# Hybrid attention encoder layer: the output projection turned round, and the second chunk's matmuls ordered by token block

## The chip, the cores and the metric

The kernel runs on one core of a Trainium2 chip. The metric is the device time of one execution in microseconds (us).

## The reference, cut to what matters

One encoder layer is applied to a prompt of 1024 tokens and to a sample of 256 tokens, each with 16 meta tokens ahead; the model width is 2048.

```python
def encoder_layer(h, norm_w, w_in, ..., w_out, rope_tabs):
    u = rms_norm(h, norm_w) @ w_in
    qa, ka, va, za, qb, kb, vb, zb = jnp.split(u, split_points(), axis=-1)
    ...
    ya = global_gqa(qa, ka, va) * jax.nn.silu(za)              # heads 0 to 7
    yb = neighbourhood_attention(qb, kb, vb, rpb) * jax.nn.silu(zb)   # heads 8 to 15
    y = jnp.concatenate([ya, yb], axis=-1) @ w_out             # 2048 x 2048
    return h + y
```

The meta tokens' rows are dropped from the output, so the output projection covers 1280 tokens.

## The kernel before

**Precision.** TensorE works on float32 numbers split in two parts, high and low (`split`, L56: ScalarE copies the high part, L58; VectorE subtracts it, L59). A product is three matmuls: high by high, high by low, low by high (L206 to L208 and L945 to L947).

**First chunk** (`chunk1`): 512 tokens, namely the sample, 240 prompt tokens and the meta tokens. For each strip of 128 columns of w_in, `strips` (L173) accumulates 16 tiles of 128 features, w as weights, tokens moving in one block of 496 or 512. Attention of the sample runs between strips. Beside it, `w_sums` (L536) computes four matrices of differences of w_out's quarters and leaves them in DRAM (`td`).

**Second chunk** (`chunk2`): the other 784 tokens in two blocks of 512 and 272. `strips` goes through four groups of four feature tiles; inside a group it takes tile by tile, inside a tile each job (strip), and inside a job both token blocks: three matmuls of 512, then three of 272. Between strips run attention blocks: global heads (`attend`, L317) and, for the local heads, four strips of 256 queries each (`attend_strip`, L412). The last strip projected is v of the last local head. Each block's result goes to DRAM by `put_y` (L300, store L315) in tensors `yd`, one a head, 128 features by 1280 tokens.

**Output projection** (`outproj`, L990). It follows Strassen's scheme in Winograd's form: seven products of half-size matrices in the order 1, 2, 5, 6, 7, 3, 4. The halves of y are the global heads and the local heads by two halves of 640 tokens; those of w_out are 1024 by 1024. Product 1 takes the global heads of the first half, product 2 the local heads of the first half. A product has eight steps, one for each 128 output features: 8 heads x 2 token blocks x 3 matmuls, 48 matmuls with w as weights and 320 tokens moving (`products`, L936). `y_load` and `y_operand` (L871, L885) bring one head's 640 tokens and split them; eight such tiles serve a product, 16 buffers (`ym`) hold two products. `w_load` and `w_operand` (L901, L912) bring and split the weights of a step two or three steps ahead. `out_sums` (L950) adds the product into the running sums U and V (`us`, `vs`) or into an output tile `o` that already holds the residual x (`x_load`, L921); `store` writes it.

**What sets the order.** All DMAs are issued by SyncE's queue (SP), in order; every engine executes its queue in order. The order of the queues is chosen ahead of the run by a list scheduler with the program order as priority. From the start of product 2 on, `in_order` (L860) pins each engine to the program's order. The last local head's four strips are emitted after steps 0 to 3 of product 1. The pools of the output projection (`us`, `raw3`, `ym`) take the memory on the right side that x of the second chunk (16 tiles of 6.25 KB a partition) and the scales beside it (6.1 KB) leave; a buffer waits for the tiles that lay there. The pools `yr`, `ysp`, `w2`, `raw2`, `vs`, `ob` take the place of the attention's pools once its last strip is done.

Of the kernel before, what the change touches and what calls it, by code (L numbers as in the profile page):

```python
# [20 lines left out]
P = 128  # L21
DM = 2048
# [24 lines left out]
TH = (NP + NS) // 2  # L47
QA, KA, VA, ZA, QB_, KB, VB, ZB = 0, 8, 10, 12, 20, 28, 36, 44
# [3 lines left out]
class Kern:  # L52
# [120 lines left out]
    def strips(self, jobs, getx):  # L173
# [4 lines left out]
        for c in range(KT // WCH):  # L178
# [21 lines left out]
            for k in range(WCH):  # L200
                kt = c * WCH + k
                x = getx(kt)
                for (wh, wl), ps, (_, blocks, _) in zip(ws, out, jobs):
                    for p, (_, n), (xh, xl) in zip(ps, blocks, x):
                        first, last = kt == 0, kt == KT - 1
                        nc.tensor.matmul(p[:, :n], wh[:, k, :], xh[:, :n], start=first, stop=False)  # L206
                        nc.tensor.matmul(p[:, :n], wh[:, k, :], xl[:, :n], start=False, stop=False)  # L207
                        nc.tensor.matmul(p[:, :n], wl[:, k, :], xh[:, :n], start=False, stop=last)  # L208
# [91 lines left out]
    def put_y(self, po, tot, zs, ydst):  # L300
# [14 lines left out]
        nc.sync.dma_start(ydst, y[:].rearrange("p (g r) -> p g r", g=4) if len(ydst.shape) == 3 else y[:])  # L315
# [220 lines left out]
    def w_sums(self):  # L536
# [6 lines left out]
        for s in range(8):  # L543
            for i in range(0, 8, WCH):
                q = {}
                for n, c, j in (("12", 8 + s, i), ("11", s, i), ("22", 8 + s, 8 + i), ("21", s, 8 + i)):
                    r = self.xr.tile([P, WCH, P], F32, tag="xr", name="wq")
                    nc.sync.dma_start(r[:], w[c][:, j:j + WCH, :])
                    q[n] = r[:]
# [7 lines left out]
                for n, p in (("11", 5), ("12", 7), ("22", 6), ("21", 4)):  # L557
                    nc.sync.dma_start(self.td[s][p][:, i:i + WCH, :], q[n])
                yield

    def chunk1(self):
# [86 lines left out]
        def run(h, q, z, k, v, vm, tab):  # L648
            k, km = k
            ydst = self.yd[h][:, NP:]  # L650
# [33 lines left out]
    def chunk2(self):  # L684
# [115 lines left out]
        def run_block(h, b, q, z, k, v, tab):  # L800
            k, km = k
            v, vm = v
            if tab is not None:
                c = slice(64 * b, 64 * b + 64)
                q, qf = q
                self.attend_strip(q, qf, strips_of(z[:])[:, :, c], k, km, v[b], vm[:], tab, b,
                                  strips_of(self.yd[h][:, :NP])[:, :, c])
# [63 lines left out]
    def y_load(self, p, k):  # L871

        def half(h, t):
            r = self.yr.tile([P, TH], F32, tag="xr", name="yr")
            self.nc.sync.dma_start(r[:], self.yd[h][:, TH * t:TH * t + TH])
            return r[:]

        if p in (1, 2, 4):
            t = self.ym.tile([P, 2, TH], F32R, tag="ym", name="ym", align_bytes=ALIGN)
            self.nc.sync.dma_start(t[:, 1, :].bitcast(F32), self.yd[k if p == 1 else 8 + k][:, TH * (p == 4):][:, :TH])  # L880
            return t
        return [half(*x) for x in {7: [(k, 0), (k, 1)],
                                   5: [(k, 1), (8 + k, 1)], 6: [(k, 0)], 3: [(8 + k, 0)]}[p]]

    def y_operand(self, p, k, r):  # L885
        nc = self.nc
        if p in (1, 2, 4):
            self.split(r[:, 0, :], r[:, 1, :], r[:, 1, :].bitcast(F32))
# [4 lines left out]
        else:  # L893
            v = self.ysum[k][:]
            a, b, op = {5: (r[0], r[-1], ALU.add), 6: (v, r[0], ALU.subtract), 3: (r[0], v, ALU.subtract)}[p]
            nc.vector.tensor_tensor(out=v, in0=a, in1=b, op=op)
        t = self.ym.tile([P, 2, TH], F32R, tag="ym", name="ym", align_bytes=ALIGN)
        self.split(t[:, 0, :], t[:, 1, :], v)
        return t

    def w_load(self, p, s):  # L901
        src = {1: lambda: self.io["w_out"][s][:, :8, :], 2: lambda: self.io["w_out"][s][:, 8:, :],
               3: lambda: self.io["w_out"][8 + s][:, 8:, :]}.get(p, lambda: self.td[s][p][:])()
        out = []
        self.nwl += 1
        for i, pool in enumerate((self.raw, (self.raw2, self.raw3)[self.nwl % 2])):
            r = pool.tile([P, WCH, P], F32, tag="raw", name="wr")
            self.nc.sync.dma_start(r[:], src[:, WCH * i:WCH * i + WCH, :])
            out.append(r)
        return out  # L910

    def w_operand(self, raws):  # L912
        ws = []
        for i, r in enumerate(raws):
            wh = self.ws[i].tile([P, WCH, P], F32R, tag="wh", name="wh")
            wl = self.ws[i].tile([P, WCH, P], F32R, tag="wl", name="wl")
            self.split(wh[:], wl[:], r[:])
            ws += [(wh[:, k, :], wl[:, k, :]) for k in range(WCH)]
        return ws

    def x_load(self, p, s):  # L921

        nc, io = self.nc, self.io
        if p not in (2, 7, 3, 4):
            return None
        o = self.ob.tile([P, TH], F32, tag="o", name="o")
        c, half = {2: (s, 0), 7: (8 + s, 1), 3: (8 + s, 0), 4: (s, 1)}[p]
        if half == 0:
            nc.sync.dma_start(o[:, :C1P], io["x1"][:, c, NS:NS + C1P])
            nc.sync.dma_start(o[:, C1P:], io["x2"][:, c, :TH - C1P])  # L930
        else:
            nc.sync.dma_start(o[:, :NP - TH], io["x2"][:, c, TH - C1P:])
            nc.sync.dma_start(o[:, NP - TH:], io["x1"][:, c, :NS])
        return o

    def products(self, ws, ys):  # L936
        nc = self.nc
        B = TH // 2
        ps = self.pq.tile([P, 2, 512], F32, tag="pq", name="pq")
        for k in range(8):  # L940
            wh, wl = ws[k]
            yh, yl = ys[k][:, 0, :], ys[k][:, 1, :]
            for b in range(2):
                o = slice(B * b, B * b + B)
                nc.tensor.matmul(ps[:, b, :B], wh, yh[:, o], start=k == 0, stop=False)  # L945
                nc.tensor.matmul(ps[:, b, :B], wh, yl[:, o], start=False, stop=False)  # L946
                nc.tensor.matmul(ps[:, b, :B], wl, yh[:, o], start=False, stop=k == 7)  # L947
        return ps[:, :, :B]

    def out_sums(self, p, s, ps, o):  # L950

        nc = self.nc

        def two(t):
            return t[:].rearrange("p (b n) -> p b n", b=2)
# [4 lines left out]
        if p == 1:  # L960
            self.U[s] = self.us.tile([P, TH], F32, tag="u", name="u")
            nc.scalar.copy(two(self.U[s]), ps)
            return None
        if p == 5:
            self.V[s] = self.vs.tile([P, TH], F32, tag="v", name="v")
            nc.scalar.copy(two(self.V[s]), ps)
            return None
        if p == 6:
            add(two(self.U[s]), ps, two(self.U[s]))
            add(self.V[s][:], self.V[s][:], self.U[s][:])  # L970
            return None
        if p in (2, 4):
            add(o[:], o[:], self.U[s][:])
            add(two(o), two(o), ps, ALU.add if p == 2 else ALU.subtract)
            return o, s, int(p == 4)
        add(o[:], o[:], self.V[s][:])
        add(two(o), ps, two(o))
        if p == 7:
            add(two(self.U[s]), ps, two(self.U[s]))
        return o, 8 + s, int(p == 7)  # L980

    def store(self, o, c, half):
        nc, io = self.nc, self.io
        if half == 0:
            nc.sync.dma_start(io["yp"][:, c, :TH], o[:])
        else:
            nc.sync.dma_start(io["yp"][:, c, TH:], o[:, :NP - TH])
            nc.sync.dma_start(io["ys"][:, c, :], o[:, NP - TH:])

    def outproj(self, end_attention):  # L990
        self.U, self.V = {}, {}
        order = (1, 2, 5, 6, 7, 3, 4)
        N = 8 * len(order)

        def step(n):
            return order[n // 8], n % 8

        yr, ys, wr, ws, x, out = {}, {}, {}, {}, {}, {}

        def get(d, n, f, *a):  # L1000
            if n not in d and n < N:
                d[n] = f(*step(n), *a)


        for n in range(8):
            yr[n] = self.y_load(*step(n))
            ys[n] = self.y_operand(*step(n), yr.pop(n))
            if n == 0:
                for i in range(2):
                    get(wr, i, self.w_load)  # L1010
                    ws[i] = self.w_operand(wr.pop(i))
        traced = None
        for n in range(N):
            p, s = step(n)
            if n == 8:
                for _ in self.blocks:
                    pass
                end_attention()
                traced = len(self.nc.cur_bb.bb.instructions)
            if n - 2 in out:  # L1020
                self.store(*out.pop(n - 2))
            get(wr, n + 2, self.w_load)
            if n > 7:
                get(wr, n + 3, self.w_load)
            if n > 7:
                get(x, n, self.x_load)
                get(x, n + 1, self.x_load)
            m = n + 8
            if n > 7 or s > 3:
                for m in ((m,) if n > 7 else (2 * n, 2 * n + 1)):  # L1030
                    if m < N:
                        ys[m] = self.y_operand(*step(m), yr.pop(m) if m in yr else self.y_load(*step(m)))
            if n > 7:
                get(yr, n + 9, self.y_load)
# [167 lines left out]
```

## Time and profile before

| | |
|---|---|
| timed runs | 2203.32, 2206.5, 2207.92 us (median 2206.5) |
| profiled execution | 2202.31 us, span 2200.5 us, TensorE clock 0.998 |
| TensorE (PE) busy | 2174.5 us, 12744 matmuls and as many weight loads |
| VectorE (DVE), ScalarE (ACT), GpSimd (POOL) busy | 1648.5, 1120.6, 518.8 us |
| matmuls of `strips` | 3456 of 512 columns, 1536 of 496, 2496 of 272 |
| matmuls of `products` | 2688 of 320 columns |
| DMA | 383.97 MB, mean 174 GB/s |

A page of the profile shows one execution: busy time of each engine, the span in 40 slices, DMA queues, the chain of work that ended last, and the costliest groups of instructions (line, engine, operation, output<-inputs, shape, count, then busy us and mean ns, then the idle time ahead and what ended it). PEld is the weight load of a matmul. Matmuls are pipelined, so their durations overlap; the time from one start to the next is read from the timeline. L206 is line 206 of the kernel.

### The profile page before, as it was taken

To read this page: it belongs to the slowest core of one execution; us is meant where nothing else is said; L and a number is where in the kernel's file an instruction comes from. 1 tells how busy PE (TensorE), PEld (TensorE's weight loads), DVE (VectorE), ACT (ScalarE), POOL (GpSimd) and SP (SyncE) were. 2 spreads that over 40 slices of the span, in tenths; PEclk is the share of its full clock that TensorE was granted. 3 is DMA by queue.
4 is the path that set the end of the run, shared out by engine and by line. 5 is a ranking of instruction groups with operands and counts; after the bars stand their busy time and mean duration, and the time that the engine had idled before them with its cause. 6 is when DMAs were issued, how large, how long until landed. Compare 5 with 4: busy or idle time off the path is not lost.

```text
span 2200.5 us, 36174 instructions
## 1 busy us (share of the span) xinstructions
PE 2174.5 (99%) x12744; PEld 1960.0 (89%) x12744; DVE 1648.5 (75%) x2967; ACT 1120.6 (51%) x2276; POOL 518.8 (24%) x249
## 2 busy tenths in 40 slices
PE   8999999999999999999999999999999999999999
PEld 7888887888878999998999999998889889999999
DVE  7687976787764999986899989777768776536743
ACT  6555544455454676665676666544444454222220
POOL 1132422222211232221333223422323311000000
PEclk9999999999999999999999999999999999999999
DMA  8767889988464334334333335644434364645663
GB/s 289 226 189 229 281 274 316 337 266 287 137 214 146 106 113 116 106 108 140 103 108 119 99 117 165 189 138 134 134 118 129 118 230 142 228 136 163 212 207 112
DMA packets 264534, 383.97 MB, mean 174 GB/s; under 512 B 45824, under 2 KB 120224, under 8 KB 264352
## 3 DMA queue, kind: packets, MB, share of 16 engines
q1 hardware_dynamic: 264352, 381.66, 54.7%
q8 instruction: 100, 1.64, 0.3%
q14 instruction: 82, 0.67, 0.1%
HBM read 281.01 MB, written 100.38 MB: 173 GB/s over the span
## 4 chain that ended last, share of the span: by engine, by line
PE 91%; DMA 3%; DVE 3%; SPq 1%; ACT 1%; issue 1%; POOL 0%; DVEq 0%; POOLq 0%; ACTq 0%
PE pp L206 20%; PE pp L208 20%; PE pp L207 20%; PE pq L946 6%; PE pq L947 6%; PE pq L945 6%; PE po L466 1%; PE po L368 1%; PE sp L434 1%; PE po L370 1%; PE sp L328 1%; PE po L369 1%; PE sp L330 1%; PE sp L329 1%; DMA wld<-wl 1%
## 5 line engine op out<-in xcount | busy, mean ns | idle before, releaser
L206 PE MATMUL pp<-x,wh 128*128 128x512 f32 (+1 forms) x2496 | 895.5, 360 | 8.8 <-ACT wh L58 7.5
L208 PE MATMUL pp<-x,wl 128*128 128x512 f32 (+1 forms) x2496 | 891.3, 357 | 0.0
L207 PE MATMUL pp<-x,wh 128*128 128x512 f32 (+1 forms) x2496 | 888.9, 356 | 0.4 <-DVE x L156 0.4
L206 PEld LDWEIGHTS pp<-x,wh 128*128 128x128 f32 x2496 | 469.6, 188 | 73.4 <-ACT wh L58 8.5
L207 PEld LDWEIGHTS pp<-x,wh 128*128 128x128 f32 x2496 | 470.6, 189 | 61.8 <-DVE x L156 1.1
L208 PEld LDWEIGHTS pp<-x,wl 128*128 128x128 f32 x2496 | 469.4, 188 | 62.1 <-DVE wl L59 0.6
L59 DVE TENSOR_TENSOR wl<-wr,wh 128x512 fp32r<-128x512 f32 (+1 forms) x402 | 299.2, 756 | 156.7 <-ACT wh L58 119.6
L58 ACT CAST wh<-wr 128x512 fp32r<-128x512 f32 (+1 forms) x402 | 239.6, 609 | 245.5 <-PE pp L207 174.4
L216 POOL PARTITION_ALL_REDUCE m<-ms x78 | 227.4, 2915 | 381.0 <-ACT ms L214 337.0
L297 POOL PARTITION_ALL_REDUCE tot<-a x80 | 176.9, 2211 | 478.0 <-DVE a L295 472.0
L945 PE MATMUL pq<-ym,wh 128*128 128x320 f32 x896 | 277.4, 310 | 5.0 <-ACT ym L58 5.0
L946 PE MATMUL pq<-ym,wh 128*128 128x320 f32 x896 | 277.9, 310 | 1.2 <-DVE ym L59 1.2
L947 PE MATMUL pq<-ym,wl 128*128 128x320 f32 x896 | 277.4, 310 | 0.2 <-DVE wl L59 0.2
L280 POOL PARTITION_ALL_REDUCE ma<-m x80 | 106.6, 1333 | 427.3 <-DVE m L278 414.4
L945 PEld LDWEIGHTS pq<-ym,wh 128*128 128x128 f32 x896 | 168.8, 189 | 6.1 <-ACT ym L58 5.9
L946 PEld LDWEIGHTS pq<-ym,wh 128*128 128x128 f32 x896 | 168.8, 188 | 1.9 <-DVE ym L59 1.9
L947 PEld LDWEIGHTS pq<-ym,wl 128*128 128x128 f32 x896 | 168.8, 188 | 0.5 <-DVE wl L59 0.5
L191 ACT CAST wh<-wr 128x512 fp32r<-128x512 f32 x132 | 81.4, 616 | 54.6 <-PE pp L207 50.9
L332 ACT COPY S<-sp 128x512 f32<-128x512 f32 x136 | 78.2, 581 | 54.4 <-PE sp L330 44.3
L59 DVE TENSOR_TENSOR pl<-S,ph 128x512 fp32r<-128x512 f32 x136 | 96.1, 719 | 10.8 <-ACT ph L58 10.5
L349 ACT ACTIVATE S<-S 128x512 f32<-128x512 f32 x136 | 84.0, 629 | 34.1 <-DVE S L348 34.1
L65 ACT ACTIVATE rs_l<-m 128x512 f32<-128x512 f32 (+1 forms) x78 | 43.7, 560 | 111.4 <-DVE m L217 109.8
(197 smaller groups left out, 3202.3 us busy)
## 6 DMA issues: line engine op xcount, KB each, us to landing
wr<-in_w_in SPq DMA_DIRECT2D x414, 256.0 KB, 3.7
wld<-wl SPq DMA_DIRECT2D x132, 256.0 KB, 4.5
wl<-wld SPq DMA_DIRECT2D x132, 256.0 KB, 3.3
wq<-in_w_out SPq DMA_DIRECT2D x64, 256.0 KB, 5.4
td<-wq SPq DMA_DIRECT2D x64, 256.0 KB, 4.6
wr<-td SPq DMA_DIRECT2D x64, 256.0 KB, 3.3
yr<-yd SPq DMA_DIRECT2D x48, 320.0 KB, 3.9
wr<-in_w_out SPq DMA_DIRECT2D x48, 256.0 KB, 3.8
```

Of the source, the lines that this page charges most:

```text
L58: self.hi = nc.scalar.copy(hi, full).ins
L59: return nc.vector.tensor_tensor(out=lo, in0=full, in1=hi.bitcast(F32), op=ALU.subtract).ins
L206: nc.tensor.matmul(p[:, :n], wh[:, k, :], xh[:, :n], start=first, stop=False)
L207: nc.tensor.matmul(p[:, :n], wh[:, k, :], xl[:, :n], start=False, stop=False)
L208: nc.tensor.matmul(p[:, :n], wl[:, k, :], xh[:, :n], start=False, stop=last)
L216: nc.gpsimd.partition_all_reduce(m2[:], ms[:], P, RED.add)
L280: nc.gpsimd.partition_all_reduce(ma[:], m1[:], P, RED.max)
L297: nc.gpsimd.partition_all_reduce(tot[:], a1[:], P, RED.add)
L349: nc.scalar.activation(s, s, AF.Exp, scale=SCALE)
L945: nc.tensor.matmul(ps[:, b, :B], wh, yh[:, o], start=k == 0, stop=False)
L946: nc.tensor.matmul(ps[:, b, :B], wh, yl[:, o], start=False, stop=False)
L947: nc.tensor.matmul(ps[:, b, :B], wl, yh[:, o], start=False, stop=k == 7)
```

## The change

The output projection is turned round. A step now makes 128 tokens by 512 output features: a slice of y (128 features of one head by 128 tokens) is the weights, and w_out moves in blocks of 512 features. A product has 5 token tiles (`NT`) x 2 feature blocks (`FB`), ten steps of 8 heads x 3 matmuls, 24 of 512 columns. y lies in DRAM as two tensors (global and local heads) by token tile, so that a tile of 128 tokens by 8 heads is one load; it is split once for two steps, in three buffers (`yo`). All of a product's w, 16 operands of 128 by 512, is held split in 16 buffers (`wm`); the next product's replace them during the last token tile. Sums, residual and output are tiles of 128 tokens by 512 features; w_out, x and the output have a layout by rows in DRAM for that. PSUM for products is four buffers of one bank instead of two of two. `w_sums` writes its four matrices in the new layout. The last local head's strips are still emitted after steps 0 to 3; the first y tile of product 2 is made ahead of the last step of product 1.

In `strips` the token block becomes the outer loop inside a group of four feature tiles: twelve matmuls of 512 for each job, then twelve of 272.

```diff
+NT = TH // P
+FB = 512
+FH = DM // 2
...
-            for k in range(WCH):
-                kt = c * WCH + k
-                x = getx(kt)
-                for (wh, wl), ps, (_, blocks, _) in zip(ws, out, jobs):
-                    for p, (_, n), (xh, xl) in zip(ps, blocks, x):
-                        first, last = kt == 0, kt == KT - 1
+            for b in range(len(jobs[0][1])):
+                for k in range(WCH):
+                    kt = c * WCH + k
+                    xh, xl = getx(kt)[b]
+                    first, last = kt == 0, kt == KT - 1
+                    for (wh, wl), ps, (_, blocks, _) in zip(ws, out, jobs):
+                        p, n = ps[b], blocks[b][1]
...
-            ydst = self.yd[h][:, NP:]
+            ydst = self.yd[h // 8][:, NP // P:, h % 8, :]
...
-            self.attend(q[:, :, c], z[:, c], keys, km, v, vm[:], self.yd[h][:, c])
+            self.attend(q[:, :, c], z[:, c], keys, km, v, vm[:], self.yd[0][:, 2 * b:2 * b + 2, h, :])
...
+    def y_load(self, p, t):
+        def half(i, h):
+            r = self.yr.tile([P, 8, P], F32, tag="yr", name="yr")
+            self.nc.sync.dma_start(r[:], self.yd[i][:, NT * h + t])
+            return r[:]
         if p in (1, 2, 4):
+            r = self.yo.tile([P, 2, 8, P], F32R, tag="yo", name="yo")
+            self.nc.sync.dma_start(r[:, 1].bitcast(F32), self.yd[p > 1][:, NT * (p == 4) + t])
+            return r
+        return [half(*x) for x in {7: [(0, 0), (0, 1)], 5: [(0, 1), (1, 1)], 6: [(0, 0)], 3: [(1, 0)]}[p]]
...
+    def w_load(self, p, j):
+        b, k = divmod(j, 8)
+        src = {1: (0, 0), 2: (8, 0), 3: (8, FH)}.get(p)
+        r = self.w.tile([P, FB], F32, tag=("wh", "wl")[j % 2], name="ww")
...
+    def w_operand(self, r):
+        w = self.wm.tile([P, 2, FB], F32R, tag="wm", name="wm", align_bytes=ALIGN)
+        self.split(w[:, 0, :], w[:, 1, :], r[:])
+        return w
...
+    def products(self, ws, y):
+        nc = self.nc
+        ps = self.pq.tile([P, FB], F32, tag="pq", name="pq")
         for k in range(8):
+            wh, wl = ws[k][:, 0, :], ws[k][:, 1, :]
+            yh, yl = y[:, 0, k, :], y[:, 1, k, :]
+            nc.tensor.matmul(ps[:], yh, wh, start=k == 0, stop=False)
+            nc.tensor.matmul(ps[:], yh, wl, start=False, stop=False)
+            nc.tensor.matmul(ps[:], yl, wh, start=False, stop=k == 7)
+        return ps[:]
...
     def outproj(self, end_attention):
...
+        N = 2 * NT * len(order)
...
+        make_y(0)
+        for j in range(8):
+            load_w(0, j)
+        for j in range(16):
+            make_w(0, j)
+            if j < 8:
+                load_w(0, 8 + j)
         traced = None
         for n in range(N):
+            p, t, b = step(n)
+            q, m = n // (2 * NT), n // 2
+            if n == 2 * NT - 1:
                 for _ in self.blocks:
                     pass
+            if n == 2 * NT:
                 end_attention()
                 traced = len(self.nc.cur_bb.bb.instructions)
+                load_y(m + 1)
             if n - 2 in out:
+                self.store(out.pop(n - 2), *step(n - 2))
+            last = t == NT - 1
+            if t == NT - 2 and b == 0:
+                for j in range(8):
+                    load_w(q + 1, j)
+            if q:
+                for i in (n, n + 1, n + 2):
+                    if i < N and i not in x:
+                        x[i] = self.x_load(*step(i))
+                load_y(m + 2)
+            if b == 0 and (q or not last):
+                make_y(m + 1)
+            if q == 0 and last and b == 1:
+                make_y(m + 1)
+            ps = self.products([ws[q, 8 * b + k] for k in range(8)], ys[m])
+            if last:
+                for k in range(8):
+                    make_w(q + 1, 8 * b + k)
+                    if b == 0:
+                        load_w(q + 1, 8 + k)
+            o = self.out_sums(p, 2 * t + b, ps, x.pop(n, None))
             if o:
                 out[n] = o
+            if n < 2 * NT:
                 next(self.blocks, None)
             if traced:
                 traced = self.in_order(traced)
...
-                pool(es_y, "pq", 2, space=PSUM, **kw)
+                pool(es_y, "pq", 4, space=PSUM, **kw)
-                for name, bufs in (("us", 8), ("raw3", 2), ("ym", 16)):
+                for name, bufs in (("us", 2 * NT), ("wm", 16), ("yo", 3)):
                     pool(es_late, name, bufs, side="right", **kw)
...
-                    for name, bufs in (("yr", 4), ("ysp", 1), ("w2", 4), ("raw2", 2), ("vs", 8), ("ob", 3)):
+                    for name, bufs in (("yr", 4), ("ysp", 1), ("vs", 2 * NT), ("ob", 5)):
                         pool(es_y, name, bufs, **kw)
...
-    outs = {"yp": (P, KT, NP), "ys": (P, KT, NS)}
+    outs = {"y": (P, 2 * NT, DM)}
```

More of the change, by code (lines that the diff above doesn't have):

```diff
@@ L893, in y_operand @@
         else:
-            v = self.ysum[k][:]
+            v = self.ysum[t][:]
             a, b, op = {5: (r[0], r[-1], ALU.add), 6: (v, r[0], ALU.subtract), 3: (r[0], v, ALU.subtract)}[p]
             nc.vector.tensor_tensor(out=v, in0=a, in1=b, op=op)
[L897 to L923, printed above, removed]
+        o = self.yo.tile([P, 2, 8, P], F32R, tag="yo", name="yo")
+        self.split(o[:, 0], o[:, 1], v)
@@ L992, in outproj @@
         order = (1, 2, 5, 6, 7, 3, 4)
-        N = 8 * len(order)
+        N = 2 * NT * len(order)
         def step(n):
-            return order[n // 8], n % 8
-        yr, ys, wr, ws, x, out = {}, {}, {}, {}, {}, {}
[L1000 to L1011, printed above, removed]
+            q, r = divmod(n, 2 * NT)
+            return order[q], *divmod(r, 2)
@@ L1045, in outproj @@
         for n in sorted(out):
-            self.store(*out[n])
+            self.store(out[n], *step(n))
     def build(self):
```

154 lines of the change are left out of this document (63 added, 91 removed).

## The prediction

> **What bounds the kernel now.** Read the page first: span, share of each engine, clock, chain.
>
> ```profile
> span 2200.5 us, 36174 instructions
> PE 2174.5 (99%) x12744; PEld 1960.0 (89%) x12744; DVE 1648.5 (75%) x2967; ACT 1120.6 (51%) x2276; POOL 518.8 (24%) x249
> ...
> PEclk9999999999999999999999999999999999999999
> ...
> PE 91%; DMA 3%; DVE 3%; SPq 1%; ACT 1%; issue 1%; POOL 0%; DVEq 0%; POOLq 0%; ACTq 0%
> ```
>
> TensorE is the bound: 91% of the chain. So the questions are what a matmul costs from start to start, and where TensorE waits. The mean durations of the groups can't be used for the first, since matmuls overlap. Take the timeline, first and last row of undisturbed runs: output projection (320 columns), first chunk (512), second chunk (three of 512, three of 272, in turn).
>
> ```profile
> 2000.03 0.31 PE L947 MATMUL pq<-ym,wl 128*128 128x320 f32 x1
> ...
> 2011.91 0.31 PE L947 MATMUL pq<-ym,wl 128*128 128x320 f32 x1
> ```
>
> ```profile
> 300.18 0.39 PE L208 MATMUL pp<-x,wl 128*128 128x512 f32 x1
> ...
> 302.90 0.39 PE L208 MATMUL pp<-x,wl 128*128 128x512 f32 x1
> ```
>
> ```profile
> 1001.18 0.39 PE L206 MATMUL pp<-x,wh 128*128 128x512 f32 x1
> ...
> 1008.60 0.39 PE L206 MATMUL pp<-x,wh 128*128 128x512 f32 x1
> ```
>
> 81 matmuls in 11.88 us are 146.7 ns for 320 columns; 12 in 2.72 us are 226.7 ns for 512. The 192 more columns cost 80.0 ns, 0.4167 ns a column (2.4 GHz), so both carry the same 13.3 ns on top of their columns. The third fence has 42 matmuls in 7.42 us, 1060 ns per three of each width; by the line just found 3 x 226.7 + 3 x 126.7 is 1060 too: taking the widths in turn costs nothing.
>
> Now the last stage by windows (columns: window, length, then busy and count of PE, PEld, DVE, ACT, POOL, clock, DMA share, GB/s).
>
> ```profile
> 1777.30:1786.60 9.30, 6.00 (x33) 4.22 (x33) 6.95 (x14) 5.62 (x11) 1.06 (x1) 1.00 0.83 270
> 1786.60:1858.40 71.80, 71.80 (x497) 71.64 (x496) 54.98 (x115) 37.96 (x75) 14.78 (x9) 1.00 0.62 207
> 1858.40:1862.30 3.90, 0.11 (x1) 0.00 (x0) 0.77 (x3) 0.72 (x1) 0.00 (x0) 1.00 0.66 256
> 1862.30:1867.00 4.70, 4.25 (x16) 4.03 (x17) 2.37 (x3) 0.72 (x2) 0.00 (x0) 0.64 0.14 54
> 1867.00:2196.60 329.60, 329.58 (x2248) 329.31 (x2246) 174.14 (x244) 80.46 (x137) 0.00 (x0) 1.00 0.56 178
> 2196.60:2200.50 3.90, 0.00 (x0) 0.00 (x0) 0.82 (x1) 0.00 (x0) 0.00 (x0) 1.00 0.23 84
> ```
>
> From 1867 to 2196.6 TensorE never waits: 2248 matmuls x 146.7 ns are the whole 329.7 us. Ahead of it two places lose time. After the second chunk the first y tiles are late; and from 1858.4 product 2 waits for the y of the last head, after which 16 matmuls take 4.7 us at a clock of 0.64 instead of 2.3 us. The chain names both:
>
> ```profile
> 1778.77 5.96 DMA ym<-yd
> 1784.75 0.73 ACT ym L58
> ...
> 1856.05 5.46 DMA ym<-yd
> 1861.53 0.73 ACT ym L58
> ```
>
> **The matmuls (gain 13.4 us).** The output projection has 7 products x 8 steps x 48 = 2688 matmuls of 320 columns; the change makes it 7 x 10 x 24 = 1680 of 512. The columns streamed are equal (860,160), so what goes is 1008 times 13.3 ns. 2688 x 146.7 ns = 394.2 us; 1680 x 226.7 ns = 380.8 us. The weights are now slices of y, 128x128 as before, and one load per matmul stays; loads were hidden behind 320 columns and stay so behind 512. That 512 columns cost the same in this stage is the one assumption; it is bounded below.
>
> The Trainium skill, "TensorE: Matmul & The Clock Gate", section "Back-to-back issue gap", puts the gap at N/2.4 + 2.5 ns, which leaves almost nothing to win by wider matmuls: 1008 x 2.5 ns, an estimate of 2.5 us. The three runs above have 13.3 ns at 320, 512 and 272 alike, so the measurement decides, and the sum goes by it.
>
> **Second chunk by token block (0, between -2 and +2 us).** Same matmuls, weights and splits; 1060 ns either way. At its start x tiles come singly, so four 512-blocks must be there before the first 272-block: up to 1 us later. At a strip's end the first block is done 12 x 127 - 3 x 127 = 1.1 us earlier.
>
> **Vector and scalar work, DMAs.** Elements split, added, loaded and stored are equal: 112 splits of 512 for w stay, 56 y splits of 640 become 35 of 1024, sums 640 x 8 become 512 x 10 per product. TensorE hides them if they are on time. put_y's store is of two 512 B pieces for each 1 KB row, on a stage where DMA queues are half idle. w_sums moves the same 2 KB rows. All 0.
>
> **The two waits, worked forward from 1777.3,** when the last strip's matmuls end (transposes and scores until about 1779.3).
>
> ```profile
> SPq L880 <- PE pp L208: 2.7, 1, 2.7
> ```
>
> ```profile
> 1780.24 0.38 SPq L490 DMA_DIRECT2D vn<-vl  x1
> ...
> 1784.80 0.32 SPq L495 DMA_DIRECT2D vn<-vl  x1
> ```
>
> ```profile
> vn<-vl SPq DMA_DIRECT2D x10, 256.0 KB, 3.3
> ...
> z<-zd SPq DMA_DIRECT2D x8, 512.0 KB, 5.8
> ```
>
> ```profile
> 1797.65 1.03 ACT L58 CAST q<-qfull 128x1024 fp32r<-128x1024 f32 x1
> ```
>
> The first y load waited for the last matmul over x, because its buffer lies where x was (first fence: SP's load, released by PE). The late pools are now 20 + 64 + 24 = 108 KB a partition; what x and its neighbour free is 16 x 6.25 + 6.1 = 106.1 KB, so one y buffer reaches into the evacuation pool. If the first y tile gets that buffer, it waits for whatever used it last: at the earliest long before 1777 (then steps start at 1779.3), at the latest the store issued at 1784.80, landing 3.3 later. I take the middle store: 1780.24 + 3.3 + 5.8 (a 512 KB load) + 1.03 (its ACT copy) = 1790.4. W's splits are off this path: most of their buffers lie over x tiles that the strip has read before.
>
> Product 1 is 10 x 24 x 226.7 ns = 54.4 us, and the four last strips with the rest of the fifth some 11 us (each 16 matmuls of 1.10 us per eight, and four small ones):
>
> ```profile
> 1820.02 1.10 PE po L466 x8
> ...
> 1852.56 0.37 SPq L315 DMA_DIRECT2D yd<-y  x1
> ```
>
> Steps 10 and 11 need token tile 0 of product 2, which strips 0 and 1 of the last head write; step 12 needs tile 1, written by strips 2 and 3. The last strip's store is at 1852.56 (second row, SP's timeline). Landing 3 us (the wait of the old chain, 1852.56 to 1856.05, is 3.5) + 5.8 + 1.03 gives a first possible step 12 at about 1862.6. By TensorE it starts at 1790.4 + 54.4 + 11 + 10.9 + 1.7 (half clock after the idle time, as at 1862.3) = 1868.4, and with an early y tile at 1855.6, so held to 1862.6 + 1.7 = 1864.3. Either way the strips' chain pins it: 1864 to 1868, middle 1866. From there 58 steps x 24 x 226.7 ns = 315.6 us, the tail as now 3.9 us (one vector add, one store): span 2185.5, and 1.8 us around the span as now (2202.31 against 2200.5): 2187.3, plus 0.7 for the changes of product below. That is 14.3 us under the profiled execution's 2202.31. The median of the runs shown is 4.2 us above that execution, so the forecast is 2206.5 - 14.3 = **2192 us**, by itself 2188 to 2196.
>
> **Changes of product (0.7 us in all, bounds 0 to 30).**
>
> ```profile
> L59 DVE TENSOR_TENSOR wl<-wr,wh 128x512 fp32r<-128x512 f32 x90 | 57.8, 684 | 0.0
> ...
> L958 DVE TENSOR_TENSOR o<-pq,o 128x640 f32<-128x640 f32 x16 | 13.2, 824 | 37.0 <-PE pq L947 37.0
> ```
>
> All 16 w buffers hold the running product, so the next one's splits start only in its last token tile, each behind the matmuls that free the buffer. The order is fixed by the program there: VectorE does the next y tile (a sum and a split of 1024, some 2.4 us), 8 w subtractions (57.8/90 = 0.64 us each, 5.1), the step's sums (2 or 3 x 0.65), 8 more (5.1), sums, the next y tile: 17 to 20 us in the 16.3 us of three steps. Behind a late y subtraction stand all w subtractions, which TensorE needs; w loads behind them hold SP's queue, and stores and x loads with it. But the first w operand is due only two steps after its buffer is free (10.9 us), half of them three steps after, and the four PSUM buffers let TensorE run past late sums. So I see it absorbed, but for a fraction of a us at the change into product 3, whose predecessor has three sums a step.
>
> **Rivals.**
> - *Both waits nearly go* (24 in 100). VectorE has 35 y splits instead of 56 and most w splits before 1777, so strips end 10 us earlier, and the y tile is early: step 12 at 1855.6, 10.4 us under 1866: 2182. For it: strips end 10.6 us apart (1820.02 above, next row), on what VectorE leaves them. Against: each is a chain of its own over four engines.
>
> ```profile
> 1830.62 1.10 PE po L466 x8
> ```
>
> - *The cost is by column, not by matmul* (11 in 100). If 512 columns from the split w buffers take 394.2/1680 = 234.6 ns, the change does not do what the count says: the forecast plus 13.4: 2205.5. For it: after attention matmuls the second chunk's 512 take 0.24 us (next fence). Against: the first chunk's 226.7. The gap rule of the Trainium skill, "TensorE: Matmul & The Clock Gate", section "Back-to-back issue gap", would come out near this rival, some 2203 us, an estimate.
>
> ```profile
> 1009.90 0.40 PE L206 MATMUL pp<-x,wh 128*128 128x512 f32 x1
> 1010.14 0.40 PE L207 MATMUL pp<-x,wh 128*128 128x512 f32 x1
> ```
>
> - *VectorE's queue stalls TensorE at every change of product* (17 in 100), the side on which it gets slower. Place: six changes, each with the 17 to 20 us in 16.3 above. If y's load is late as well (5.8 us is a median), the w splits are pushed behind it and TensorE waits 5 us each time, 30 us in all, half clock included: 2222. It decides from (14.3 + 4.4)/6 = 3.1 us per change.
>
> **How the numbers follow.** A measurement of this kernel can tell about 0.2%, 4.4 us. Forecast 48 in 100, 2192. Faster: forecast and first rival, 0.72; same: the second, 0.11; slower: the third, 0.17. The range goes from under the first rival (2180) over the second to 2209; the third lies above it, and 3 in 100 below.
>
> **What would show it.** Right: 1680 matmuls of 128x512 in pq, 226 to 228 ns from start to start, no idle TensorE from step 12 on, and about 12 us lost ahead of it. Wrong: windows at the changes of product with idle TensorE released by ACT or DVE of wm; a first y load later than 1788; a pitch over 230 ns; second-chunk groups of six that differ from 1060 ns.

## The result, and the profile after

The changed kernel takes 2197.75 us, the median of 7 runs (2196.61 to 2198.34); the kernel before, run beside it, 2204.11 us (2201.57 to 2207.92, 7 runs). The ratio is 0.9968, 95% interval 0.9956 to 0.9979: 6.4 us faster, where 14.3 us were forecast. The profiled execution took 2197.35 us, its span is 2195.5.

The page of the changed kernel: span, busy time, clock, and the chain by engine.

```profile
span 2195.5 us, 34052 instructions
PE 2166.0 (99%) x11736; PEld 1879.9 (86%) x11736; DVE 1650.8 (75%) x2956; ACT 1125.7 (51%) x2259; POOL 519.8 (24%) x249
...
PEclk9999999999999999999999999999999989999999
...
PE 96%; DMA 2%; DVE 1%; ACT 1%; issue 0%; SPq 0%; DVEq 0%
```

1008 matmuls are gone, as counted (12744 to 11736), and TensorE bounds the kernel even more. Where the 5.0 us between the two spans came from is read from three landmarks in the timeline: the last strip matmul of the first chunk, the last one of the second, and the end. Before:

```profile
613.03 0.38 PE L208 MATMUL pp<-x,wl 128*128 128x496 f32 x1
...
1777.13 0.29 PE L208 MATMUL pp<-x,wl 128*128 128x272 f32 x1
```

After:

```profile
608.09 0.38 PE L212 MATMUL pp<-x,wl 128*128 128x496 f32 x1
...
1768.07 0.28 PE L212 MATMUL pp<-x,wl 128*128 128x272 f32 x1
```

| stage (us) | before | after | difference | forecast |
|---|---|---|---|---|
| start to the last strip matmul of the first chunk | 613.0 | 608.1 | -4.9 | 0 |
| from there to the last strip matmul of the second | 1164.1 | 1160.0 | -4.1 | 0 |
| from there to the end | 423.4 | 427.4 | **+4.0** | about -15 |

So the time was won where the prediction put nothing, and the stage that was to win lost. Two things are to be seen in that stage. The first is what a matmul costs; two rows of the timeline, nine matmuls apart:

```profile
1998.35 0.39 PE L935 MATMUL pq<-wm,yo 128*128 128x512 f32 x1
...
2000.45 0.39 PE L935 MATMUL pq<-wm,yo 128*128 128x512 f32 x1
```

Nine in 2.10 us are 233.3 ns, not 226.7. The second is its beginning; windows of the changed kernel, the columns as in the prediction:

```profile
1769.50:1791.10 21.60, 7.65 (x38) 6.43 (x37) 17.24 (x37) 13.07 (x27) 2.86 (x2) 0.60 1.00 357
1791.10:1835.00 43.90, 43.41 (x210) 36.07 (x210) 31.61 (x70) 18.42 (x39) 12.44 (x8) 1.00 0.33 98
1835.00:2191.00 356.00, 356.00 (x1528) 286.41 (x1527) 190.63 (x257) 95.01 (x140) 0.00 (x0) 1.00 0.54 182
```

TensorE is busy for 7.65 of 21.6 us, at a clock of 0.60. After 1835 it never waits, and 1528 x 233.3 ns are the whole 356 us: the wait before step 12 is gone, and the six changes of product cost nothing. The waits of TensorE from 1760 to 2190 (waited in total, times, longest), SP's queue and ScalarE's copy of the first y tile show what the first wait is made of:

```profile
PE sp L438 <- DMA ww<-in_w_out: 11.5, 1, 11.5
PE tp L491 <- ACT vl L493: 2.2, 1, 2.2
PE pq L937 <- DVE yo L62: 0.5, 1, 0.5
```

```profile
1768.30 0.80 SPq L912 DMA_DIRECT2D ww<-in_w_out  x2
...
1779.16 0.33 SPq L791 DMA_DIRECT2D qfull<-q2d  x1
1779.84 3.82 SPq L912 DMA_DIRECT2D ww<-in_w_out  x6
1783.75 1.10 SPq L884 DMA_DIRECT2D yo<-yd  x2
```

```profile
1789.68 1.05 ACT L61 CAST yo<-yo 128x1024 fp32r<-128x1024 f32 x1 [1.50 <-DMA yo<-yd]
```

The first y load is issued at 1783.75, behind 22 loads of w: all 16 of product 1 and six of product 2's. Some of them wait for buffers that the strips' weights or the w splits hold. The 11.5 us of TensorE end at the scores of an attention strip (L438), which stand ahead of the products in its queue and whose last load of q (1779.16) stands among the w loads as well. (The view names a load of w there, though the scores read q and k alone.) The y tile holds the products a little longer: it has landed only when ScalarE's copy of it starts, at 1789.68, and the products start at 1791.1, 23.0 us after the last strip matmul.

### The profile page after: what moved, and what is told of

Same layout as the page of the kernel before. It is cut to its first block, busy times and chain, and to the rows that moved or that the text cites. A ratio compares the mean times of both kernels' runs of the same rounds, so it can differ in the third digit from the quotient of the medians.

```text
span 2195.5 us, 34052 instructions
## 1 busy us (share of the span) xinstructions
PE 2166.0 (99%) x11736; PEld 1879.9 (86%) x11736; DVE 1650.8 (75%) x2956; ACT 1125.7 (51%) x2259; POOL 519.8 (24%) x249
## 4 chain that ended last, share of the span: by engine, by line
PE 96%; DMA 2%; DVE 1%; ACT 1%; issue 0%; SPq 0%; DVEq 0%
PE pp L210 21%; PE pp L211 21%; PE pp L212 21%; PE pq L937 6%; PE pq L936 6%; PE pq L935 6%; PE po L470 2%; PE po L372 1%; PE po L374 1%; PE sp L332 1%; PE sp L438 1%; PE po L373 1%; PE sp L334 1%; PE sp L333 1%; DMA ww<-in_w_out 0%; PE tp L491 0%
## 5 line engine op out<-in xcount | busy, mean ns | idle before, releaser
L62 DVE TENSOR_TENSOR wl<-wr,wh 128x512 fp32r<-128x512 f32 (+1 forms) x290 | 214.5, 742 | 129.6 <-ACT wh L61 106.8
L61 ACT CAST wh<-wr 128x512 fp32r<-128x512 f32 (+1 forms) x290 | 175.1, 608 | 227.4 <-PE pp L211 215.8
L937 PE MATMUL pq<-wm,yo 128*128 128x512 f32 x560 | 223.2, 399 | 0.5 <-DVE yo L62 0.5
L936 PE MATMUL pq<-wm,yo 128*128 128x512 f32 x560 | 220.8, 394 | 0.0
L935 PE MATMUL pq<-wm,yo 128*128 128x512 f32 x560 | 220.5, 394 | 0.0
L936 PEld LDWEIGHTS pq<-wm,yo 128*128 128x128 f32 x560 | 105.1, 188 | 26.9
L937 PEld LDWEIGHTS pq<-wm,yo 128*128 128x128 f32 x560 | 105.1, 188 | 25.3 <-DVE yo L62 1.1
L935 PEld LDWEIGHTS pq<-wm,yo 128*128 128x128 f32 x560 | 105.1, 188 | 24.6
L61 ACT CAST ph<-S 128x512 fp32r<-128x512 f32 x136 | 83.3, 613 | 34.1 <-PE po L373 33.8
L352 DVE TENSOR_TENSOR S<-S,ma 128x512 f32<-128x512 f32 x136 | 97.2, 772 | 3.9 <-POOL ma L284 3.9
```

Of the source, the lines that this page charges most:

```text
L61: self.hi = nc.scalar.copy(hi, full).ins
L62: return nc.vector.tensor_tensor(out=lo, in0=full, in1=hi.bitcast(F32), op=ALU.subtract).ins
L352: nc.vector.tensor_tensor(out=s, in0=s, in1=mb, op=ALU.subtract)
L935: nc.tensor.matmul(ps[:], yh, wh, start=k == 0, stop=False)
L936: nc.tensor.matmul(ps[:], yh, wl, start=False, stop=False)
L937: nc.tensor.matmul(ps[:], yl, wh, start=False, stop=k == 7)
```

## The experiments

Theory: (a) the products' matmuls lose the expected gain because of where their operands lie, (b) the start is late because of the y load's place in SP's queue, (c) the second chunk gains by the token blocks. Rivals: (a') the cost goes by column in this stage, wherever things lie; (b') the w operands hold the start; (c') the difference of the chunks is one of executions. In the table "final stage" runs from the last strip matmul to the end of the profiled span. The offsets are the start addresses of the y and w operand tiles, as the allocator placed them, modulo 256 bytes. The pitch (ns) is the mean time from one matmul's start to the next, without waits. The kernels were timed on several occasions, each beside the kernel before, whose median then lay between 2200.50 and 2204.11 us; a difference of a few us between two rows is therefore read from the stages of the traces as well.

| kernel | median us (runs) | before beside it | ratio to before (95%) | final stage | y, w offset | pitch in the products |
|---|---|---|---|---|---|---|
| changed | 2197.75 (7) | 2204.11 | 0.9968 (0.9956 to 0.9979) | 427.4 | 32, 128 | 233.3 |
| y aligned | 2195.34 (8) | 2203.26 | 0.9970 (0.9960 to 0.9979) | 425.7 | 0, 128 | 232.4 |
| y where x lay | 2189.73 (5) | 2203.26 | 0.9942 (0.9931 to 0.9954) | 420.0 | 32, 128 | 233.3 |
| aligned and early | 2190.34 (5) | 2203.26 | 0.9945 (0.9933 to 0.9956) | 420.5 | 128, 0 | 232.4 |
| both on 256 | 2178.19 (4) | 2203.08 | 0.9889 (0.9872 to 0.9905) | 409.3 | 0, 0 | 226.7 |
| both on 128 | 2180.58 (2) | 2201.26 | 0.9908 (0.9889 to 0.9926) | 410.6 | 128, 128 | 226.8 |
| changed, both on 256 | 2187.57 (5) | 2200.50 | 0.9942 (0.9928 to 0.9955) | 417.8 | 0, 0 | 226.7 |
| before, strips by block | 2198.00 (12) | 2203.26 | 0.9977 (0.9968 to 0.9987) | 423.6 | | 146.7 (320) |
| changed, widths in turn | 2200.86 (11) | 2202.48 | 0.9995 (0.9986 to 1.0004) | 427.7 | 32, 128 | 233.3 |
| before, y on 256 | 2201.42 (11) | 2201.26 | 1.0004 (0.9995 to 1.0013) | 422.6 | | 146.7 (320) |

**The weights alone put on a boundary** (in both places where y tiles are made).

```diff
- self.yo.tile([P, 2, 8, P], F32R, tag="yo", name="yo")
+ self.yo.tile([P, 2, 8, P], F32R, tag="yo", name="yo", align_bytes=ALIGN)
```

> The y tiles, now the weights of the output projection, are put on a boundary of 128 bytes (they lie at 118528 in place of 118560, a multiple of 256); nothing else moves, and each engine's order stays. Theory: a matmul of 512 columns costs 233.3 ns from start to start there, and not 226.7, because its weights lie 32 bytes past a multiple of 64. Then a group of three takes 680 ns in place of 700, and 1680 x 6.7 = 11 us go: about 2186.5 against 2197.75 of the change. Rival (cost by column): the weights' place has no part in it; a group stays at 700 ns and the time at about 2197.7.

```profile
1998.77 0.40 PE L935 MATMUL pq<-wm,yo 128*128 128x512 f32 x1
...
2000.86 0.39 PE L935 MATMUL pq<-wm,yo 128*128 128x512 f32 x1
```

Nine matmuls in 2.09 us, 232.2 here; 697 ns a group over the stage. The theory as stated fell: 1.7 us of the final stage went, not 11. But the rhythm changed, from 231, 232, 237 ns on end to a round of seven (241, 232, 231, 232, 228, 230, 233), so the address does act on TensorE.

**y where x lay.**

```diff
- for name, bufs in (("us", 2 * NT), ("wm", 16), ("yo", 3)):
+ for name, bufs in (("wm", 16), ("yo", 3), ("us", 2 * NT)):
```

> Only the order of the three late pools is turned: the sums U, which are written after the first product, lie lowest, where one y buffer reached into the second chunk's evacuation buffers, and the y buffers lie wholly where x was. y keeps its offset of 32 bytes. Theory: the products began late (1791.1) because the first y load was issued only at 1783.75, behind 16 w loads. With the y load ahead of most of these the products begin near 1780, and the final stage shrinks from 426.0 to some 416 us: about 2188. Rival: the w operands (16 loads and splits, the last split at 1784.9) and half clock set the start as much as y, so TensorE waits inside the first step in place of ahead of it: 2195 to 2198.

SP's queue and TensorE's timeline of this kernel:

```profile
1768.09 0.33 SPq L912 DMA_DIRECT2D ww<-in_w_out  x1
1768.47 0.42 SPq L884 DMA_DIRECT2D yo<-yd  x1
```

```profile
1775.17 0.80 PE L935 MATMUL pq<-wm,yo 128*128 128x512 f32 x1 [3.67 <-ACT yo L61]
1775.76 0.63 PE L936 MATMUL pq<-wm,yo 128*128 128x512 f32 x1
1779.41 0.80 PE L937 MATMUL pq<-wm,yo 128*128 128x512 f32 x1 [3.02 <-DVE yo L62]
1780.00 0.63 PE L935 MATMUL pq<-wm,yo 128*128 128x512 f32 x1
1780.43 0.63 PE L936 MATMUL pq<-wm,yo 128*128 128x512 f32 x1
```

The y load moved 15 us ahead and the products begin 7.3 us after the last strip matmul. The final stage shrinks by 7.4 us, the run by 8.0 (by 7.2 when each kernel is set against the kernel before beside it). Theory (b) holds; a part of (b') too: ahead of the first y tile VectorE splits seven w operands and does three steps of an attention strip, so that TensorE waits another 3.02 us, and at half clock a matmul takes 427 ns until 1782.6. The Trainium skill, "TensorE: Matmul & The Clock Gate", section "What's actually happening", says that idleness throttles TensorE to 1.2 GHz; 512 columns at that would be 426.7 ns, an estimate by that page, and the rows agree.

**Before, with the strips by token block alone** (the loop of the change's diff in the kernel before).

> The kernel before with the second half of the change alone: matmuls of the strips by token block, the output projection as it was. Theory: a group of three of 512 and three of 272 columns takes 1060 ns when the widths alternate (231, 224, 231, 126, 124, 124) and 680 + 374 = 1054 by block; 832 such pairs are 5 us: 2199 against 2204.1. Rival (the prediction's term): no gain, 2204, and the 4 us that the second chunk lost between the two traces are a difference between executions.

Timeline of this kernel: six matmuls of 272 columns between the first two rows, three of 512 between the last two, and the landmarks.

```profile
1007.80 0.29 PE L207 MATMUL pp<-x,wh 128*128 128x272 f32 x1
...
1008.55 0.40 PE L207 MATMUL pp<-x,wh 128*128 128x512 f32 x1
...
1009.25 0.39 PE L207 MATMUL pp<-x,wh 128*128 128x512 f32 x1
...
1009.93 0.39 PE L207 MATMUL pp<-x,wh 128*128 128x512 f32 x1
```

```profile
614.27 0.38 PE L209 MATMUL pp<-x,wl 128*128 128x496 f32 x1
...
1774.38 0.28 PE L209 MATMUL pp<-x,wl 128*128 128x272 f32 x1
```

5.3 us faster, as the theory has it. From landmark to landmark 1160.1 us, against 1164.1 before; three narrow matmuls take 375 ns and three wide ones 680, together 1055 where the alternated six took 1060.

**Aligned and early** (both edits above, y on top of the late pools).

```diff
- for name, bufs in (("us", 2 * NT), ("wm", 16), ("yo", 3)):
+ for name, bufs in (("yo", 3), ("wm", 16), ("us", 2 * NT)):
- self.yo.tile([P, 2, 8, P], F32R, tag="yo", name="yo")
+ self.yo.tile([P, 2, 8, P], F32R, tag="yo", name="yo", align_bytes=ALIGN)
```

> The y tiles on the top of the late pools (128 past a multiple of 256), the w operands on multiples of 256, the sums U lowest: both edits of the first two experiments at once. If the weights' place and the late first y load both cost what is thought, 11 + 10 us go: about 2177. If only the weights: 2186.5. If only the start: 2188. If neither: 2197.7. A group of three at 680 with the start unchanged, or the other way round, tells which.

Only the start counts: 2190.3 us, with a group at 697 ns. This placing put w on 256 and y at 128, the converse of the first experiment, with the same 232.4 ns.

**Four arms.** Edit (weights low in the partition: a pool `yq` on the other side):

```diff
+ b = k % 2 if p in (5, 3) else 0
...
+ three = ((yh, wh), (yl, wh), (yh, wl)) if p == 7 else ((yh, wh), (yh, wl), (yl, wh))
...
+ pool, n = (self.yq, "yq") if p in (6, 3) else (self.yo, "yo")
```

> One look at what sets the 233 ns of the products' matmuls; the late pools as in the second experiment, and each product another arm. Products 1, 2 and 4 as they were. Product 5: the steps of the inner sum go by turns to two PSUM banks, as the strips do after each group of three, and only one bank is evacuated (half of its sum is left out). Product 6: the y tiles (weights) lie at 30 to 46 KB of a partition, low as the strips' weights do (11 to 27 KB), in place of 139 to 163 KB among the w operands. Product 7: the order in a group is yh x wh, yl x wh, yh x wl, so that the weights change at each matmul. Product 3: both banks and the low y tiles (half of the sum left out). Theory A (one bank for 24 matmuls on end costs 6.7 ns each): 680 ns a group in products 5 and 3, 700 elsewhere. Theory B (weights and moving data in one region): 680 in products 6 and 3. Theory C (the cost is by column in this stage, whatever lies where): 697 to 700 in all.

Mean pitch, without waits, in products 1, 2, 5, 6, 7, 3, 4: 233.4, 233.3, 233.4, 233.3, 233.4, 232.4, 233.3 ns. No arm comes near 226.7 ns, so neither banks nor region nor order within a group is the cause. A and B fell. One thing more moved than was meant: the low y tiles of products 6 and 3 start at offset 0, as in the first experiment. Product 3 has the pitch of that experiment, 232.4 ns, in its round of seven; product 6 has 233.3 in another rhythm, 229 and 238 ns by turns. So the same pair of offsets can give either.

**The changed kernel with the widths in turn** (its strips with the loop of before).

> The changed kernel with the strips' matmuls in their old order, widths in turn; output projection and the sums of w_out as changed. Theory: the token blocks are worth 4 to 5 us in the second chunk (groups of six at 1060 ns again in place of 1054), and the new layout of w_out's sums 2 to 4 us in the first chunk, where VectorE waited 11.8 us for their loads before and 0 in the changed kernel; the turned output projection is worth nothing by itself. Then 2202, between the change's 2197.75 and before's 2203. Rival: the first chunk's gain belongs to chance between executions; then about 2206, slower than before.

Its landmarks:

```profile
606.79 0.38 PE L211 MATMUL pp<-x,wl 128*128 128x496 f32 x1
...
1771.52 0.29 PE L211 MATMUL pp<-x,wl 128*128 128x272 f32 x1
```

The second chunk takes 1164.7 us again, so the token blocks are all of its gain; the first chunk keeps its gain, 606.8 against 613.0. The output projection turned round, together with the first chunk's gain from its new layout, is worth nothing that can be measured (0.9995): the final stage is 4.3 us longer than in the kernel before.

**Widths.**

```diff
+ width = {1: 512, 2: 496, 5: 480, 6: 448, 7: 416, 3: 384, 4: 256}[p]
+ n = width if k else FB
+ wh, wl = ws[k - b][:, 0, :n], ws[k - b][:, 1, :n]
```

> One look, pools as in the second experiment. The products' matmuls (but for the first group of each step) stream n of the 512 columns, another n in each product: 512, 496, 480, 448, 416, 384, 256 in the order 1, 2, 5, 6, 7, 3, 4; what lies beyond n is left out of the sums. In token tiles 1 and 3 two neighbouring groups of three also read the same w operand and go to two PSUM banks, as the strips do with one x tile for two jobs; half of the sum is left out there. Theory 1 (the 20 ns on top of the columns belong to 512 in this stage, where 320 columns had 13.3 ns): they fall to 13.3 ns within the narrower products, 480 at 213.3 ns. Theory 2 (they belong to this arrangement, y as weights and w moving): 20 ns at each width, 480 at 220 ns, 256 at 126.7. Theory 3 (the strips stay at 13.3 ns because two groups share their moving data): token tiles 1 and 3 at 226.7 ns in product 1, 0, 2 and 4 at 233.3.

On top of n x 0.4167 ns stay 20.3, 17.8, 19.8, 18.6, 19.9, 16.6 ns at 512, 496, 480, 448, 416, 384, the same to 0.3 ns in tiles that share w and in tiles that don't; only 256 columns have 13.3 (in tiles 1 and 3; in the others waits are mixed in). So theory 2 in the main, but for 256: the cost is there at most widths of this stage, not at 512 columns alone, and theories 1 and 3 fell. That left the addresses: in no kernel so far had both operands been on 256.

**Both on 256, and the arms again.**

```diff
- tag="yo", name="yo")
+ tag="yo", name="yo", align_bytes=2 * ALIGN)
...
- tag="wm", name="wm", align_bytes=ALIGN)
+ tag="wm", name="wm", align_bytes=2 * ALIGN)
```

> The second experiment's kernel with both operands of the products on a multiple of 256 bytes, as both operands of the strips are; so far only one of the two was (y at 0 and w at 128 past it in the first experiment, y at 128 and w at 0 in the fourth). Theory: the strips' 13.3 ns on top of the columns need both there; then 680 ns a group of three, 1680 x 6.7 = 11 us less than the second experiment's 2189.7: about 2179. Rival (the arrangement costs 20 ns wherever its operands lie): 697 to 700 ns, 2188 to 2190.

> One look, both operands on multiples of 256 bytes. Products 1, 2 and 4 as they are; product 5 in two PSUM banks by turns; product 6 in two banks and with y low in the partition (both: half of the sum left out); product 7 takes yh x wh, yh x wl and again yh x wh, so that the weights are the same three times (the term yl x wh left out); product 3 takes yh x wh twice and yl x wh, so that the moving data are the same three times (the term yh x wl left out). If the place on 256 is the cause, all arms have 680 ns. If it needs a second condition of the strips, the arm that meets it has 680: banks 5 and 6, the low place 6. If a change of weights or of moving data costs the 6.7 ns, 7 or 3 is lower. If none, 697 to 700 everywhere.

The kernel takes 2178.2 us, 11.5 under the second experiment's and by the theory's number, with 680 ns a group. In the arms 226.7 to 226.8 ns, without waits, everywhere behind product 1: the gain needs no second condition, and changing weights or moving data costs nothing.

**Both on 128** (the pool order of "aligned and early" without the alignment).

> The changed kernel with the y tiles on top of the late pools and the sums lowest: both operands of the products lie 128 bytes past a multiple of 256 (nothing is asked to be on 256). If it is the common offset that counts, a group of three takes 680 ns and the time is near 2179. If each operand must lie on a multiple of 256, 690 to 700 ns and 2188 to 2191.

```profile
1998.36 0.39 PE L935 MATMUL pq<-wm,yo 128*128 128x512 f32 x1
...
2000.40 0.39 PE L935 MATMUL pq<-wm,yo 128*128 128x512 f32 x1
```

Nine in 2.04 us are 226.7 ns. It is the common offset that counts: 0 and 0 or 128 and 128 have 13.3 ns on top of the columns, a difference of 96 has 20.0, one of 128 has 19 or, in one arm, 20.

**Before, y on 256.**

```diff
- name="ym", align_bytes=ALIGN)
+ name="ym", align_bytes=2 * ALIGN)
```

> The kernel before with the y tiles, there the moving operand, on multiples of 256 bytes in place of 128 past one; the w tiles (weights) lie on 256 already, and each engine's order is the same. If the rule holds for that arrangement too, the 320-column matmuls lose some of their 13.3 ns: at 11 ns, which the strips' 272 columns have by block (374 ns for three), 2688 x 2 = 5 us, 2198. If 13.3 ns is the floor at 320 columns, 440 ns a group as before and 2203.

No change: 440 ns a group, now evenly 146 to 147 where single matmuls lay between 145 and 149. At 320 columns 13.3 ns is what a matmul costs with either offset, so the kernel before lost nothing by its placing.

**The change with nothing but the offsets mended** (the diff of "both on 256", pools in the changed kernel's order).

> The changed kernel with both operands of the products on multiples of 256 bytes and nothing else: the pools in its own order, each engine's order the same. It undoes what the matmul term of the prediction missed, by itself. Theory: 680 ns a group of three from the first product on, 1680 x 6.7 = 11 us less than the change's 2197.75, the late start at 1791 unchanged: about 2186.5. Rival: with the late start left in, the faster products only run into another wait (the w operands at the changes of product), and half or less of the 11 us is seen: 2192 or more.

```profile
1998.35 0.39 PE L935 MATMUL pq<-wm,yo 128*128 128x512 f32 x1
...
2000.39 0.39 PE L935 MATMUL pq<-wm,yo 128*128 128x512 f32 x1
```

These are nine in 2.04 us, and the kernel takes 2187.57 us. From the first product to the end 393.9 us against the changed kernel's 404.4: 10.5 of the 11.2 us are seen. The start stays late (23.9 us after the last strip matmul). The whole time says it less sharply: 10.2 us under the changed kernel, but 6.6 when each is set against the kernel before beside it, which was 3.6 us faster on this occasion.

## Why the prediction was half right

- *Matmuls, 13.4 us: the step that failed.* The count was right and so was 226.7 ns for well-placed operands. "That 512 columns cost the same in this stage is the one assumption" did not hold: 233.3 ns, and 394.2 - 1680 x 0.2333 = 2.3 us were won; a pitch over 230 ns was one of the prediction's own signs of being wrong. The rival "by column" had the number (234.6) but not the reason: with the offsets alike the full term appears. The prediction's 2.5 us by the Trainium skill, "TensorE: Matmul & The Clock Gate", section "Back-to-back issue gap", came near the 2.3 by luck: the section gives that formula for a matmul in isolation, and in this stream 20.0 ns lay on top of the columns, not 2.5. What the trace of before could not show is that its 512-column strips have both operands at offset 0 (the low part of x for 272 columns lies at 128); its products, at 128 and 0, pay nothing for it at 320 columns.
- *Second chunk by token block, 0 (-2 to +2): mis-sized.* It is worth 3.3 to 4.5 us, from landmark to landmark in the eight kernels that have it. 3 x 226.7 + 3 x 126.7 = 1060 was a coincidence of two errors: by themselves three of 272 take 374, and within the alternation the wide ones take 686 (231, 224, 231) and the narrow ones 374 (126, 124, 124). The cost of taking turns was there to be read in the single starts.
- *Vector and scalar work, DMAs, 0: missed the first chunk.* Eight kernels with the new layout of w_out and its sums end the first chunk at 606.8 to 609.6, three with the old one at 613.0 to 614.4. The waits of VectorE, 20 to 620 us, of the kernel before:

```profile
DVE wl L59 <- DMA wq<-in_w_out: 11.8, 3, 4.9
```

  VectorE stands in its queue 11.8 us for the loads of the w sums, with splits behind it; in the other two kernels with the old layout 10.3 and 8.3, in the changed kernel not at all, in the other seven with the new layout 1.2 to 6.4. TensorE's own waits up to 610 us add up to 11.7 to 12.7 us with the old layout and to 7.9 to 9.5 with the new one, which is the larger part of the gain. The order of each queue in this chunk is the same before and after, and the loads land sooner (5.1 us in place of 5.4 in the median). That these loads are the whole cause is not shown: the changed kernel, where VectorE never waits for them, ends the chunk at 608.1, the one with the widths in turn, where it waits 4.6 us, at 606.8. Why the loads land sooner was not tried.
- *First wait, y at 1790.4.* Measured 1791.1, but for another reason, and from a chunk that ended 9 us sooner: 23.0 us after the last strip matmul in place of 13.1. The buffer that reaches into the evacuation pool was the cause, as the step had it, and the second experiment shows it. It did not act by a store's landing; the load simply stood behind 22 w loads in SP's queue (the second experiment's expectation has 16). That the date agrees to 0.7 us is luck: after the last strip matmul the error is some 10 us.
- *Second wait, step 12 at 1864 to 1868.* Step 12 began at 1866.7 with no wait. The last strip's store was issued at 1836.36, 16 us earlier than before, so the first rival was right about this wait and wrong about the other. (The prediction's own terms, 1852.56 + 3 + 5.8 + 1.03, give 1862.4 and not 1862.6; nothing hangs on it.)
- *Changes of product, 0.7 us.* They cost nothing measurable; the third rival is out.

Final stage by these terms, 427.4 in place of 408.4: 9.9 us for the late start and 9.3 for the pitch from step 12 on (58 x 24 x 6.67 ns) are together the 19 us. Between the two, from the first product to step 12, it took the 75.6 us that the forecast's dates (1790.4 to 1866) leave; the pitch cost 1.9 us there too, and the 1.7 us of half clock that the forecast had did not come. The 9 us that the chunks gave repaid half of the 19, by terms that the forecast had at zero. That the kernel came out within 6 us of the forecast, 2197.75 against 2192, is luck to that extent: the stage that was to win 15 us lost 4.

## What to carry to other kernels

When a transposed product swaps which tile is stationary and which is moving, look at where the two tiles start: here a common offset modulo 256 bytes was worth 10.5 us of a stage of 427, without an instruction moved. When pools are laid over freed ones, put the tile that is needed first where memory is free first, since the order of a queue follows from it. A duration read as "the same line through two points" is to be checked against the start of each single matmul.

The version with y where x lay and both operands on 256 runs in 2178.19 us, 0.9889 of the kernel before (0.9872 to 0.9905) and 19.6 us under the change.

## What the runs showed of the hardware

A matmul of 512 columns by 128 weights in this fp32 mode costs 226.7 ns from start to start where its two operands start at the same offset modulo 256 bytes, 232.4 (in one arm 233.3) where the offsets differ by 128, and 233.3 where they differ by 96. At the difference of 96 the cost showed at 384 columns and more, and not at 256; at 320 columns, in the kernel before, a difference of 128 cost nothing. The Trainium skill, "SBUF — State Buffer", section "Operand start alignment", asks for a start at a multiple of the element size and says that this is "about legality, not speed", of runs that timed nothing; all the placings here obey it, and the speed differs by 3%. Which part of TensorE the offset acts on, and what it does at other differences, stays open.

The cost also depends on what ran just before. After other matmuls have come between, the first chunk's 512s (both operands at offset 0; kernel before, from 131.2 and 242.3 us on) have 11 to 23 ns, 18 in the mean, on top of their columns for about eight matmuls and then settle at 13.3, for as long as nothing intervenes; at unequal offsets the products kept 19 to 20 ns for 300 us and more.
